# Matmul pieces of 256 and 260 columns in place of equal pieces, results contiguous in PSUM

## The chip, the core and the metric

The kernel runs on one core of one Trainium2 chip. Its engines are TensorE (PE, matmuls into PSUM), VectorE (DVE), ScalarE (ACT), GpSimd (POOL) and SyncE (SP, which issues most DMAs). The metric is the device time of one execution in microseconds (us), the median of three runs.

## What is computed

One layer of a hybrid decoder for 1024 prompt tokens and 8 sample tokens, 1032 token columns in all, model width 1024. Cut to its products:

```python
xn = rmsnorm(x, norm_mix_w)
sc_b, sc_c, sc_x, z, xbc, dt_raw, q, gates = split(xn @ w_in)      # 12320 columns
y_a = (sc_b * conv3(sc_c * sc_x)) @ w_sc_out                       # gated convolution
y_b = group_rmsnorm(ssd(conv4(xbc), dt) * silu(z)) @ w_ssm_out     # state-space scan
y_c = attention(q, mem_k, mem_v) @ w_attn_o                        # 256 memory tokens
x   = x + (g_a*y_a + g_b*y_b + g_c*y_c) @ w_merge_o                # g = sigmoid(gates)
x   = x + (silu(rmsnorm(x) @ w_gate) * (rmsnorm(x) @ w_up)) @ w_down   # hidden width 2816
y   = rmsnorm(x)
```

New caches, convolution histories and scan states are outputs too.

## The kernel before

Activations are kept transposed: 128 features on the partitions, the 1032 tokens as columns. In a product a 128x128 block of weights is the stationary operand and token columns are the moving one. Every fp32 operand is split into a high and a low part of the type fp32r, and a product is three matmuls: high by high, high by low, low by high. PSUM tiles are declared here in banks of 512 fp32 per partition, and each matmul of this kernel writes into one bank.

There are two ways to multiply.

*Plain blocks.* `gemm` (L195 on) makes one block of 128 output features for all 1032 tokens: over 8 values of k, three products each, and for each product three matmuls of CW = 344 columns, one into each bank of a tile of three (`ps[:, n, :CW]`, L214). `flat(ps)` reads the result as three runs of 344, and the SBUF operand beside it is cut the same way by `t3`. It serves two blocks of z, the eight of q and the 32 output projections (`out_part`, and the loop at L1784 on).

*Strassen blocks.* Most of `w_in`, gate, up and most of down go by pairs of output blocks as 2x2 Strassen products with 7 multiplications (`strassen`, L313 on). The second dimension of the 2x2 form is the token axis: the 1032 tokens are two halves of HT = 516. `st_prod` (L256) makes one product: 4 values of k, three products, and for each two matmuls of HC = 258 columns (L262), the first into one bank and the second into the next. The sums of token blocks (`xforms`, `forms`) are made ahead; `forms` tiles hold two halves of 516 side by side, so a half starts 0 or 2064 bytes into its tile. ACT and DVE take each result out of PSUM (`put`, L329 and L331; L364, L368, L377, L379, L384; and the callers' last step), reading it as two runs of 258 with `hv` and cutting the SBUF operand alike with `h3`.

The merge (L1865) and the part of down that is left over from the pairs (L2075) use plain sums over k, but by halves of 516, so also two matmuls of 258. In the merge's last tile (half 1, m = 7) the two pieces have a PSUM tile each: first all 24 matmuls of the first piece run, then all 24 of the second, and each is added to the residual when it is done.

Order of the work: one product follows the other on PE in program order. Small steps of other work are put into queues (`pend`, run by `tick`) and taken at fixed points between products: the scan (L1003 to L1085), the sample tokens' states (L944 to L950), the attention. The stages are: norm, transposes and the first blocks (to 60 us), z, gates, xBC and the short convolution as Strassen blocks (to 990 us), the scan and the attention between plain blocks of q and the output projections (to 1651 us), the merge (to 1745 us), the feed-forward part (to about 2390 us), and the last rows. The file names weights blocks after their use: X for xBC, C and B for the short convolution, G for gates, Z for z, g and u for gate and up.

```python
T = 1024
TT = T + NS            # 1032
CW = TT // NCH         # 344
HT = TT // 2           # 516
HC = HT // 2           # 258
```

Of the kernel before, what the change touches and what calls it, by code (L numbers as in the profile page):

```python
# [11 lines left out]
AF = mybir.ActivationFunctionType  # L12
# [31 lines left out]
def tile_kernel(ctx: ExitStack, tc, a, o):  # L44
# [150 lines left out]
    def gemm(w, acts, name, width=P, off=0):  # L195

        hi, lo = w
        ps = mm_ps(name)
        nk = len(acts)
        n = int(pace[0] + pace[1])  # L200
        pace[1] += pace[0] - n
        marks = [nk * i // n for i in range(n)]
        between = seam.pop() if seam else None
        for k, (ah, al) in enumerate(acts):
            if between is not None:
                between(k)
            if k == 1 and owed:
                owed.pop()()
            for _ in range(marks.count(k)):
                tick()  # L210
            ks = slice(k * width + off, k * width + off + P)
            for i, (wt, x) in enumerate(((hi, ah), (hi, al), (lo, ah))):
                for n in range(NCH):
                    PE.matmul(  # L214
                        ps[:, n, :CW], wt[:, ks], x[:, n * CW : (n + 1) * CW],
                        start=(k == 0 and i == 0), stop=(k == nk - 1 and i == 2),
                    )
        return ps
# [15 lines left out]

    def h3(t):
        return t.rearrange("p (n c) -> p n c", n=2)

    def hv(ps):
        return ps[:, :2, :HC]

# [15 lines left out]
    def st_prod(forms, ps, w, off, f, start):  # L256
        for kt in range(4):
            xh, xl = forms[f][kt]
            ks = slice(off + kt * P, off + (kt + 1) * P)
            for i, (wt, x) in enumerate(((w[0], xh), (w[0], xl), (w[1], xh))):  # L260
                for n in range(2):
                    PE.matmul(  # L262
                        ps[:, n, :HC], wt[:, ks], x[:, n * HC : (n + 1) * HC],
                        start=(start and kt == 0 and i == 0), stop=(kt == 3 and i == 2),
                        skip_group_check=True,
                    )

    def st_early(blocks, forms):


        for first in range(0, len(blocks), 3):
            held = []
            for i, (src1, nm, out, keep) in enumerate(blocks[first : first + 3]):
                wA = st_split(st_raw(src1, f"{nm}Er"), f"{nm}E")
                ps = st_ps(f"m{i}", f"{nm}e")
                o1 = out()
                st_prod(forms, ps, wA, 0, "B11", True)
                S.copy(h3(o1[:, HS[1]]), hv(ps))
                held.append((wA, ps, o1, keep))
            for wA, ps, o1, keep in held:  # L280
                st_prod(forms, ps, wA, 512, "B21", False)
                S.copy(h3(o1[:, HS[0]]), hv(ps))
                keep(o1)
# [29 lines left out]
    def strassen(src1, src2, forms, nm, sums, outs, early=None, after_t3=None, ready=None, hook=None, add=False, begun=None, mid=None):  # L313
# [47 lines left out]
        if early is None:  # L361
            put(o12, pa)
            prod(pc, wA, 512, "B21", True)
            V.tensor_tensor(h3(o11), hv(pc), h3(o11), op=ALU.add)  # L364
        else:
            S.copy(o21, o12)
            V.tensor_sub(o22, o22, o12)
            freed[0] = V.tensor_tensor(h3(o12), hv(pa), h3(o12), op=ALU.add).ins  # L368
        if mid is not None:
# [5 lines left out]
        if after_t3 is not None:  # L375
            after_t3()
        V.tensor_tensor(h3(o22), h3(o22), hv(pa), op=ALU.subtract)  # L377
        prod(pb, wT, 512, "B22", False)
        V.tensor_tensor(h3(o12), h3(o12), hv(pb), op=ALU.subtract)  # L379
        tick()  # L380
        wD = st_split(raw2[:, 512:], f"{nm}D", 512)
        prod(pa, wD, 0, "T4", False)
        if early is not None:
            V.tensor_tensor(h3(o21), hv(pa), h3(o21), op=ALU.add)  # L384
            return o21
# [411 lines left out]
    def sc_pairs(ct):  # L797

        accs = []
        for i in (ct, ct + 1):  # L800
# [12 lines left out]
            ux = u[:, 2 : 2 + TT]  # L813
            V.scalar_tensor_tensor(h3(ux[:, HS[0]]), pa, -1.0, h3(c[:, HS[0]]), op0=ALU.mult, op1=ALU.mult)
            V.tensor_mul(ux[:, HS[1]], ux[:, HS[1]], c[:, HS[1]])
# [16 lines left out]
        SY.dma_start(sc_d[ct], a1)  # L832
        V.scalar_tensor_tensor(h3(a2[:, HS[0]]), pa, -1.0, h3(a2[:, HS[0]]), op0=ALU.mult, op1=ALU.mult)
        V.tensor_mul(a2[:, HS[1]], a2[:, HS[1]], o[1][:, HS[1]])
        SY.dma_start(sc_d[ct + 1], a2)

    def q_step(i):
        def s():
            ps = proj(C_Q + i * P, f"q{i}")
            t = ev_tile(f"q{i}")  # L840
            S.activation(t3(t), flat(ps), AF.Copy, scale=QS)
# [17 lines left out]
    def xbc_pair(c1, c2, after_t3=None):  # L859
# [10 lines left out]
        xbc_conv(c1, us[0], f"x{c1}")  # L870
        S.activation(h3(us[1][:, 3 : 3 + HT]), pa, AF.Copy, scale=-1.0)  # L871
        xbc_conv(c2, us[1], f"x{c2}")

    def z_step(i):
        ps = proj(C_Z + i * P, f"z{i}")
        t = ev_tile(f"z{i}")
        S.activation(t3(t), flat(ps), AF.Silu)
        S.dma_start(zs_d[i], t[:, :TT])

    def plain_pair(col, dst, i, nm, func, hook=None, after_t3=None):  # L880
# [13 lines left out]
        S.activation(os[1][:, HS[1]], os[1][:, HS[1]], func)  # L894
        ins = S.activation(h3(os[1][:, HS[0]]), pa, func, scale=-1.0).ins
        S.dma_start(dst[i + 1], os[1][:, :TT])
# [573 lines left out]
    def out_part(i, m, w, src, nxt):  # L1470
# [14 lines left out]
        if i == 0:  # L1485
            V.tensor_mul(t3(gt), flat(ps), t3(gt))
            owed.append(lambda: SY.dma_start(mg_d[m], gt[:, :TT]))
        elif i == 1:
            t = ev_tile(f"yr{nm}")
            S.copy(t3(t), flat(ps))  # L1490
            S.dma_start(yr_d[m], t[:, :TT])
        else:
            V.tensor_tensor(t3(t), flat(ps), t3(t), op=ALU.add)  # L1493
            V.tensor_mul(t[:, :TT], t[:, :TT], gt[:, :TT])
# [289 lines left out]
    for m in range(KD):  # L1784
# [10 lines left out]
        V.tensor_add(merged[m], merged[m], yg[:, :TT])  # L1795
        V.tensor_mul(t3(gt), flat(ps), t3(gt))  # L1796
        V.tensor_add(merged[m], merged[m], gt[:, :TT])
# [49 lines left out]
    for half in range(2):  # L1847
        sq = ev_tile(f"sq{half}")
        for m in range(KD):
# [7 lines left out]
            def merge_part(out, ns):  # L1857
                for k, (ah, al) in enumerate(mg):
# [3 lines left out]
                    for i, (wt, x) in enumerate(((wh, ah), (wh, al), (wl, ah))):  # L1862
                        for n in ns:
                            c = half * HT + n * HC
                            PE.matmul(  # L1865
                                out[:, n - ns[0], :HC], wt[:, ks], x[:, c : c + HC],
                                start=(k == 0 and i == 0), stop=(k == KD - 1 and i == 2),
                            )

            if half == 1 and m == KD - 1:  # L1870

                for n in range(2):
                    ps = sm_ps(f"pm{half}{m}{n}")
                    merge_part(ps.unsqueeze(1), (n,))
                    c = slice(n * HC, (n + 1) * HC)
                    V.tensor_tensor(t[:, c], ps[:, :HC], xt[:, c], op=ALU.add)
            else:
                ps = mm_ps(f"pm{half}{m}")
                merge_part(ps, (0, 1))
                V.tensor_tensor(h3(t), hv(ps), h3(xt[:, :HT]), op=ALU.add)  # L1880
            if m == 0:
# [65 lines left out]
    def hidden_pair(nm, j, j2):  # L1947
# [18 lines left out]
        )  # L1966
        return o[0], o[1], pa if e is None else h3(pa)

# [6 lines left out]
    for n, (j, j2) in enumerate(pairs):  # L1975
        s1, s2, pa = hidden_pair("g", j, j2)
        S.activation(s1, s1, AF.Silu)
        S.activation(s2[:, HS[1]], s2[:, HS[1]], AF.Silu)
        S.activation(h3(s2[:, HS[0]]), pa, AF.Silu, scale=-1.0)
# [3 lines left out]
        V.scalar_tensor_tensor(h3(s2[:, HS[0]]), pa, -1.0, h3(s2[:, HS[0]]), op0=ALU.mult, op1=ALU.mult)  # L1983
        if j2 != j + 4:
# [53 lines left out]
    def down_pairs(part, fs, begun):  # L2038
        for m in range(0, KD, 2):
# [4 lines left out]
            )  # L2044
            o21 = h3(x2[m + 1][:, HS[0]])
            V.tensor_tensor(o21, o21, pa, op=ALU.subtract)
# [7 lines left out]
    for part, js in enumerate(([0], [9, 10])):  # L2054
# [10 lines left out]
        for m in range(KD):  # L2065
            if not part:
                x2[m] = big(f"x3_{m}")
            for half in range(2):
                ps = st_ps(tags[(2 * m + half) % 3], f"pd{part}{m}{half}")
                for k, (ah, al) in enumerate(hl):  # L2070
                    ks = slice(k * cols + m * P % cols, k * cols + m * P % cols + P)
                    wh, wl = ws[m * P // cols]
                    for i, (wt, x) in enumerate(((wh, ah), (wh, al), (wl, ah))):
                        for n in range(2):
                            PE.matmul(  # L2075
                                ps[:, n, :HC], wt[:, ks], x[:, half * HT + n * HC : half * HT + (n + 1) * HC],
                                start=(k == 0 and i == 0), stop=(k == len(hl) - 1 and i == 2),
                            )
                t = h3(x2[m][:, HS[half]])
                if part:  # L2080
# [186 lines left out]
```

## Time and profile before

| | us |
|---|---|
| time, median of 3 runs | 2445.45 (2445.1 to 2446.07) |
| span of the profiled execution | 2443.0 |
| median above the span | 2.45 |

No other time is listed for the profiled execution than its span, from the first to the last instruction. In the views, L262 is line 262 of the kernel; a row of the timeline has the start, the length, the engine, the line and what is written from what, with the shape of stationary and moving operand; a row of the chain has the start, the length and what it consists of; a row of the busy view by stretch has the stretch, its length, then busy us and (x instructions) of each engine, the granted clock, the share of the DMA engines and GB/s. The length of a matmul in the records includes its way through the array, and neighbours overlap.

### The profile page before, as it was taken

The page shows a single profiled execution, that of the slowest core. Times are in us where ns is not written, and L with a number is a line of the kernel's source. Part 1 is how long each engine was busy: PE and PEld are TensorE (multiplying, and loading weights), DVE is VectorE, ACT ScalarE, POOL GpSimd, SP SyncE. Part 2 cuts the span into 40 slices and gives each one's busy share as a digit, 9 for nine tenths or more (in the row PEclk, how much of TensorE's full clock was granted, in tenths as well). Part 3 has the DMA queues.
Part 4 walks back from the last instruction along what each step waited for, and adds up shares of the span by engine and source line. Part 5 has one row for each costly group of instructions (what it writes and reads, how often), then busy time and mean ns, then how long its engine had stood idle before and what let it go on. Part 6 is the DMA issues. An engine that isn't in the chain of part 4 may idle for free.

```text
span 2443.0 us, 45185 instructions
## 1 busy us (share of the span) xinstructions
PE 2416.7 (99%) x18716; PEld 2343.5 (96%) x18716; DVE 1613.6 (66%) x2597; ACT 1093.6 (45%) x1740; POOL 107.3 (4%) x163
## 2 busy tenths in 40 slices
PE   8999999999999999999999999999999999999998
PEld 6999999999999999998898998999999999999998
DVE  6744677777777676568687773554777655567955
ACT  6633555455453543646555542213543333343423
POOL 0000000000000000212112000000000000000000
PEclk9999999999999999999999999999999999999999
DMA  6354423444353345768887797855445333354622
GB/s 210 128 156 159 135 81 112 139 139 130 104 160 114 100 139 165 234 206 273 259 283 219 258 342 236 281 191 157 156 160 173 106 91 109 87 180 150 191 86 80
DMA packets 357717, 407.94 MB, mean 167 GB/s; under 512 B 16271, under 2 KB 277503, under 8 KB 357504
## 3 DMA queue, kind: packets, MB, share of 16 engines
q1 hardware_dynamic: 334374, 341.79, 45.1%
q10 hardware_dynamic: 23137, 63.26, 6.8%
q8 instruction: 147, 2.41, 0.4%
q14 instruction: 59, 0.48, 0.1%
HBM read 288.85 MB, written 116.38 MB: 166 GB/s over the span
## 4 chain that ended last, share of the span: by engine, by line
PE 89%; DMA 5%; DVE 3%; ACT 2%; issue 1%; SPq 0%; ACTq 0%; DVEq 0%
PE po L214 12%; PE pm L1865 4%; PE ps_q L214 3%; PE pss L1072 1%; PE py L1059 1%; PE ps_z L214 1%; PE po L1051 1%; PE G16m L262 1%; PE G22m L262 1%; PE Z2m L262 1%; PE Z14m L262 1%; PE C1m L262 1%; PE G20m L262 1%; PE C7m L262 1%; PE G12m L262 1%
## 5 line engine op out<-in xcount | busy, mean ns | idle before, releaser
L1003 ACT ACTIVATE r<-r,acum 128x128 f32<-128x128 f32 x256 | 79.2, 391 | 3.8 <-DMA r<-ac_d 3.1
L792 DVE SCALAR_TENSOR_TENSOR ax<-u,prm,ax 128x1024 f32<-128x1024 f32 x44 | 56.3, 1281 | 0.0
L944 ACT ACTIVATE st<-st,es 128x128 f32<-128x128 f32 x128 | 41.2, 391 | 20.9 <-DMA st<-in_state_ssm_dram 12.9
L1036 POOL TENSOR_TENSOR xdd<-xdt,decst 128x512 f32<-128x512 f32 x32 | 34.4, 1074 | 286.5 <-DVE xdt L1032 280.7
L1030 DVE TENSOR_TENSOR r<-r,cbm 128x1024 f32<-128x1024 f32 x32 | 39.1, 1223 | 4.3 <-ACT r L1005 2.4
L946 DVE SCALAR_TENSOR_TENSOR st<-sr,dts,st 128x128 f32<-128x128 f32 x128 | 40.1, 345 | 0.4
L1055 DVE TENSOR_TENSOR y<-po,ea 128x512 f32<-128x512 f32 x28 | 19.3, 690 | 31.0 <-PE po L1051 30.9
L1072 PE MATMUL pss<-xdd,bT 128*128 128x512 f32 x64 | 34.4, 619 | 2.0 <-ACT bT L1029 2.0
L950 DVE SCALAR_TENSOR_TENSOR sr<-st,sr 128x128 f32<-128x128 f32 x128 | 35.3, 285 | 1.1
L1493 DVE TENSOR_TENSOR yr<-po,yr 128x1032 f32<-128x1032 f32 x8 | 9.9, 1232 | 39.1 <-PE po L214 39.1
L1059 PE MATMUL py<-r,xdt 128*64 128x128 f32 x512 | 35.0, 279 | 0.0
L1005 ACT ACTIVATE r<-r 128x1024 f32<-128x1024 f32 x32 | 33.9, 1058 | 0.7
L1085 POOL TENSOR_TENSOR s<-s,cdec 128x512 f32<-128x512 f32 x28 | 33.2, 1185 | 0.7 <-DVE s L1078 0.4
L1880 DVE TENSOR_TENSOR x<-pm,xT 128x516 f32<-128x516 f32 x15 | 10.4, 693 | 33.3 <-PE pm L1865 33.3
L1796 DVE TENSOR_TENSOR gt<-po,gt 128x1032 f32<-128x1032 f32 x8 | 9.9, 1234 | 32.7 <-PE po L214 32.7
L1059 PEld LDWEIGHTS py<-r,xdt 128*64 128x64 f32 x512 | 27.3, 136 | 4.2 <-issue 0.9
L1051 PE MATMUL po<-bc,s 128*128 128x128 f32 x224 | 29.5, 274 | 0.0
L1051 PEld LDWEIGHTS po<-bc,s 128*128 128x128 f32 x224 | 28.3, 191 | 0.0
L795 DVE SCALAR_TENSOR_TENSOR ax<-u,prm,ax 128x1032 f32<-128x1032 f32 x22 | 28.3, 1287 | 0.0
L1596 DVE SCALAR_TENSOR_TENSOR kc<-kc,qb 128x256 f32<-128x256 f32 x64 | 23.8, 419 | 6.5 <-DMA qb<-qs_d 6.5
L1608 ACT ACTIVATE pr<-psa,mx 128x256 f32<-128x256 f32 x32 | 14.9, 471 | 29.2 <-DVE mx L1606 29.2
L789 ACT ACTIVATE ax<-u,prm 128x1024 f32<-128x1024 f32 x22 | 27.4, 1246 | 1.2 <-ACT u L871 0.4
(9245 smaller groups left out, 9047.2 us busy)
## 6 DMA issues: line engine op xcount, KB each, us to landing
r<-ac_d SPq DMA_DIRECT2D x32, 512.0 KB
gt_d<-G ACTq DMA_DIRECT2D x24, 516.0 KB
gt<-gt_d SPq DMA_DIRECT2D x24, 516.0 KB
xs_d<-ax ACTq DMA_DIRECT2D x22, 516.0 KB
zs<-zs_d SPq DMA_DIRECT2D x16, 516.0 KB
yb_d<-x SPq DMA_DIRECT2D x16, 516.0 KB
in<-yb_d SPq DMA_DIRECT2D x16, 516.0 KB
st<-in_state_ssm_dram SPq DMA_DIRECT2D x32, 256.0 KB
```

Of the source, the lines that this page charges most:

```text
L214: PE.matmul(ps[:, n, :CW], wt[:, ks], x[:, n * CW : (n + 1) * CW], start=(k == 0 and i == 0), stop=(k == nk - 1 and i == 2),)
L262: PE.matmul(ps[:, n, :HC], wt[:, ks], x[:, n * HC : (n + 1) * HC], start=(start and kt == 0 and i == 0), stop=(kt == 3 and i == 2), skip_g ...
L792: V.scalar_tensor_tensor(acc[:, :T], u[:, j : j + T], w[j], acc[:, :T], op0=ALU.mult, op1=ALU.add)
L944: S.activation(st[:, i], st[:, i], AF.Copy, scale=es[:, g * 4 + i, b : b + 1])
L946: V.scalar_tensor_tensor(st[:, i], rb, dts[:, g * 4 + i, b : b + 1], st[:, i], op0=ALU.mult, op1=ALU.add)
L950: V.scalar_tensor_tensor(rb, st[:, i], 1.0, rc, op0=ALU.mult, op1=ALU.mult, accum_out=ys[:, g * 4 + i, b : b + 1],)
L1003: S.activation(r[:, j, :], r[:, j, :], AF.Relu, scale=-1.0, bias=acum[:, c, h : h + 1])
L1030: V.tensor_tensor(r, r, bc(cbm.unsqueeze(1), [P, HPG, P]), op=ALU.mult)
L1051: PE.matmul(po[:, t * P : (t + 1) * P], state["s"][:, t * P : (t + 1) * P], bcg[1][:, cs], start=True, stop=True,)
L1059: PE.matmul(py[hp : hp + 64, (h // 2) * P : (h // 2 + 1) * P], xdt[:, h * 64 : (h + 1) * 64], r[:, (h % 2) * 4 + h // 2, :], start=True, s ...
L1072: PE.matmul(pss, bT, xdd, start=True, stop=True)
L1865: PE.matmul(out[:, n - ns[0], :HC], wt[:, ks], x[:, c : c + HC], start=(k == 0 and i == 0), stop=(k == KD - 1 and i == 2),)
```

## The change

Halves of 516 tokens become matmuls of 256 and 260 columns. Their results lie side by side in PSUM: the first in columns 256 to 511 of a bank, the second in columns 0 to 259 of the next, so that 516 columns follow one another without a gap. Plain blocks become matmuls of 260, 512 and 260 columns; their results lie in columns 252 to 511 of the first bank, the whole second bank and columns 0 to 259 of the third, also without a gap. ACT and DVE read each result as one run of 516 or 1032 columns, and the SBUF operands beside it are no longer cut into pieces. In the merge's last tile the two pieces are 256 and 260 columns, still in a PSUM tile each.

```diff
+    THIRDS = ((252, 0, 260), (512, 260, 772), (1024, 772, TT))
+
     def flat(ps):
-        return ps[:, :, :CW]
-
-    def t3(t, lo=0):
-        return t[:, lo : lo + TT].rearrange("p (n c) -> p n c", n=NCH)
+        return ps.rearrange("p n c -> p (n c)")[:, 252 : 252 + TT]
+
+    def thirds(ps, x):
+        f = ps.rearrange("p n c -> p (n c)")
+        for at, lo, hi in THIRDS:
+            yield f[:, at : at + hi - lo], x[:, lo:hi]
...
             for i, (wt, x) in enumerate(((hi, ah), (hi, al), (lo, ah))):
-                for n in range(NCH):
-                    PE.matmul(
-                        ps[:, n, :CW], wt[:, ks], x[:, n * CW : (n + 1) * CW],
-                        start=(k == 0 and i == 0), stop=(k == nk - 1 and i == 2),
-                    )
+                for po, xc in thirds(ps, x):
+                    PE.matmul(po, wt[:, ks], xc, start=(k == 0 and i == 0), stop=(k == nk - 1 and i == 2))
...
-    def h3(t):
-        return t.rearrange("p (n c) -> p n c", n=2)
+    HALF = ((0, 256), (256, HT))
 
     def hv(ps):
-        return ps[:, :2, :HC]
+        return ps.rearrange("p n c -> p (n c)")[:, 256 : 256 + HT]
+
+    def halves_of(ps, x, at=0):
+        f = hv(ps)
+        for lo, hi in HALF:
+            yield f[:, lo:hi], x[:, at + lo : at + hi]
...
             for i, (wt, x) in enumerate(((w[0], xh), (w[0], xl), (w[1], xh))):
-                for n in range(2):
+                for po, xc in halves_of(ps, x):
                     PE.matmul(
-                        ps[:, n, :HC], wt[:, ks], x[:, n * HC : (n + 1) * HC],
-                        start=(start and kt == 0 and i == 0), stop=(kt == 3 and i == 2),
+                        po, wt[:, ks], xc, start=(start and kt == 0 and i == 0), stop=(kt == 3 and i == 2),
                         skip_group_check=True,
                     )
...
             if add:
-                V.tensor_tensor(h3(o), hv(ps), h3(o), op=ALU.add)
+                V.tensor_tensor(o, hv(ps), o, op=ALU.add)
             else:
-                S.copy(h3(o), hv(ps))
+                S.copy(o, hv(ps))
...
-                for n in range(2):
-                    ps = sm_ps(f"pm{half}{m}{n}")
-                    merge_part(ps.unsqueeze(1), (n,))
-                    c = slice(n * HC, (n + 1) * HC)
-                    V.tensor_tensor(t[:, c], ps[:, :HC], xt[:, c], op=ALU.add)
+                for n, (lo, hi) in enumerate(HALF):
+                    ps = sm_ps(f"pm{half}{m}{n}")[:, : hi - lo]
+                    merge_part([ps], (n,))
+                    V.tensor_tensor(t[:, lo:hi], ps, xt[:, lo:hi], op=ALU.add)
...
-                        for n in range(2):
-                            PE.matmul(
-                                ps[:, n, :HC], wt[:, ks], x[:, half * HT + n * HC : half * HT + (n + 1) * HC],
-                                start=(k == 0 and i == 0), stop=(k == len(hl) - 1 and i == 2),
-                            )
+                        for po, xc in halves_of(ps, x, half * HT):
+                            PE.matmul(po, wt[:, ks], xc, start=(k == 0 and i == 0), stop=(k == len(hl) - 1 and i == 2))
```

Every other edit drops `h3` or `t3` around an operand of an eviction. The sums of squares (L1816) and the group means (L1173) keep pieces of 258 and 344.

More of the change, by code (lines that the diff above doesn't have):

```diff
@@ L277, in st_early @@
                 st_prod(forms, ps, wA, 0, "B11", True)
-                S.copy(h3(o1[:, HS[1]]), hv(ps))
+                S.copy(o1[:, HS[1]], hv(ps))
                 held.append((wA, ps, o1, keep))
@@ L281, in st_early @@
                 st_prod(forms, ps, wA, 512, "B21", False)
-                S.copy(h3(o1[:, HS[0]]), hv(ps))
+                S.copy(o1[:, HS[0]], hv(ps))
                 keep(o1)
@@ L363, in strassen @@
             prod(pc, wA, 512, "B21", True)
-            V.tensor_tensor(h3(o11), hv(pc), h3(o11), op=ALU.add)
+            V.tensor_tensor(o11, hv(pc), o11, op=ALU.add)
         else:
@@ L367, in strassen @@
             V.tensor_sub(o22, o22, o12)
-            freed[0] = V.tensor_tensor(h3(o12), hv(pa), h3(o12), op=ALU.add).ins
+            freed[0] = V.tensor_tensor(o12, hv(pa), o12, op=ALU.add).ins
         if mid is not None:
@@ L376, in strassen @@
             after_t3()
-        V.tensor_tensor(h3(o22), h3(o22), hv(pa), op=ALU.subtract)
+        V.tensor_tensor(o22, o22, hv(pa), op=ALU.subtract)
         prod(pb, wT, 512, "B22", False)
-        V.tensor_tensor(h3(o12), h3(o12), hv(pb), op=ALU.subtract)
+        V.tensor_tensor(o12, o12, hv(pb), op=ALU.subtract)
         tick()
@@ L383, in strassen @@
         if early is not None:
-            V.tensor_tensor(h3(o21), hv(pa), h3(o21), op=ALU.add)
+            V.tensor_tensor(o21, hv(pa), o21, op=ALU.add)
             return o21
@@ L840, in s @@
             t = ev_tile(f"q{i}")
-            S.activation(t3(t), flat(ps), AF.Copy, scale=QS)
+            S.activation(t[:, :TT], flat(ps), AF.Copy, scale=QS)
             G.tensor_copy(qs[:, i, :], t[:, T:TT])
@@ L870, in xbc_pair @@
         xbc_conv(c1, us[0], f"x{c1}")
-        S.activation(h3(us[1][:, 3 : 3 + HT]), pa, AF.Copy, scale=-1.0)
+        S.activation(us[1][:, 3 : 3 + HT], pa, AF.Copy, scale=-1.0)
         xbc_conv(c2, us[1], f"x{c2}")
@@ L876, in z_step @@
         t = ev_tile(f"z{i}")
-        S.activation(t3(t), flat(ps), AF.Silu)
+        S.activation(t[:, :TT], flat(ps), AF.Silu)
         S.dma_start(zs_d[i], t[:, :TT])
@@ L1485, in out_part @@
         if i == 0:
-            V.tensor_mul(t3(gt), flat(ps), t3(gt))
+            V.tensor_mul(gt[:, :TT], flat(ps), gt[:, :TT])
             owed.append(lambda: SY.dma_start(mg_d[m], gt[:, :TT]))
@@ L1489, in out_part @@
             t = ev_tile(f"yr{nm}")
-            S.copy(t3(t), flat(ps))
+            S.copy(t[:, :TT], flat(ps))
             S.dma_start(yr_d[m], t[:, :TT])
         else:
-            V.tensor_tensor(t3(t), flat(ps), t3(t), op=ALU.add)
+            V.tensor_tensor(t[:, :TT], flat(ps), t[:, :TT], op=ALU.add)
             V.tensor_mul(t[:, :TT], t[:, :TT], gt[:, :TT])
@@ L1795, in tile_kernel @@
         V.tensor_add(merged[m], merged[m], yg[:, :TT])
-        V.tensor_mul(t3(gt), flat(ps), t3(gt))
+        V.tensor_mul(gt[:, :TT], flat(ps), gt[:, :TT])
         V.tensor_add(merged[m], merged[m], gt[:, :TT])
@@ L1862, in merge_part @@
                     for i, (wt, x) in enumerate(((wh, ah), (wh, al), (wl, ah))):
-                        for n in ns:
-                            c = half * HT + n * HC
+                        for n, po in zip(ns, out):
+                            lo, hi = HALF[n]
                             PE.matmul(
-                                out[:, n - ns[0], :HC], wt[:, ks], x[:, c : c + HC],
+                                po, wt[:, ks], x[:, half * HT + lo : half * HT + hi],
                                 start=(k == 0 and i == 0), stop=(k == KD - 1 and i == 2),
@@ L1870, in tile_kernel @@
             if half == 1 and m == KD - 1:
-                for n in range(2):
-                    ps = sm_ps(f"pm{half}{m}{n}")
-                    merge_part(ps.unsqueeze(1), (n,))
-                    c = slice(n * HC, (n + 1) * HC)
-                    V.tensor_tensor(t[:, c], ps[:, :HC], xt[:, c], op=ALU.add)
+                for n, (lo, hi) in enumerate(HALF):
+                    ps = sm_ps(f"pm{half}{m}{n}")[:, : hi - lo]
+                    merge_part([ps], (n,))
+                    V.tensor_tensor(t[:, lo:hi], ps, xt[:, lo:hi], op=ALU.add)
             else:
                 ps = mm_ps(f"pm{half}{m}")
-                merge_part(ps, (0, 1))
-                V.tensor_tensor(h3(t), hv(ps), h3(xt[:, :HT]), op=ALU.add)
+                merge_part([hv(ps)[:, lo:hi] for lo, hi in HALF], (0, 1))
+                V.tensor_tensor(t, hv(ps), xt[:, :HT], op=ALU.add)
             if m == 0:
@@ L1966, in hidden_pair @@
         )
-        return o[0], o[1], pa if e is None else h3(pa)
+        return o[0], o[1], pa
     PARTS = (1, 11)
@@ L2044, in down_pairs @@
             )
-            o21 = h3(x2[m + 1][:, HS[0]])
+            o21 = x2[m + 1][:, HS[0]]
             V.tensor_tensor(o21, o21, pa, op=ALU.subtract)
@@ L2073, in tile_kernel @@
                     for i, (wt, x) in enumerate(((wh, ah), (wh, al), (wl, ah))):
-                        for n in range(2):
-                            PE.matmul(
-                                ps[:, n, :HC], wt[:, ks], x[:, half * HT + n * HC : half * HT + (n + 1) * HC],
-                                start=(k == 0 and i == 0), stop=(k == len(hl) - 1 and i == 2),
-                            )
-                t = h3(x2[m][:, HS[half]])
+                        for po, xc in halves_of(ps, x, half * HT):
+                            PE.matmul(po, wt[:, ks], xc, start=(k == 0 and i == 0), stop=(k == len(hl) - 1 and i == 2))
+                t = x2[m][:, HS[half]]
                 if part:
```

10 lines of the change are left out of this document (5 added, 5 removed).

## The prediction

> **What bounds the kernel now.** I read first the busy shares and the shares of the chain of work that ended last.
>
> ```profile
> span 2443.0 us, 45185 instructions
> ...
> PE 2416.7 (99%) x18716; PEld 2343.5 (96%) x18716; DVE 1613.6 (66%) x2597; ACT 1093.6 (45%) x1740; POOL 107.3 (4%) x163
> ...
> PEclk9999999999999999999999999999999999999999
> ...
> PE 89%; DMA 5%; DVE 3%; ACT 2%; issue 1%; SPq 0%; ACTq 0%; DVEq 0%
> ```
>
> PE is busy for 99% of the span at the full granted clock, and makes up 89% of the chain. A busy PE need not be a PE at its peak, so I then read the chain in order of time, where an unbroken PE piece (start, length, tile, line, matmuls) means that nothing else held PE up, and the longest wait of PE.
>
> ```profile
> 645.34 20.29 PE X8m L262 x168
> 665.63 20.29 PE G8m L262 x168
> ...
> 1571.92 79.69 PE po L214 x503
> ```
>
> ```profile
> PE ps_B L593 <- ACT xnh L519: 2.8, 3, 1.5
> ```
>
> One Strassen block (7 products of 24 matmuls, 168 in all) follows the next without a gap, each 20.29 us long whether it feeds a convolution (X8) or a gate (G8). PE's longest total wait is 2.8 us, in the opening. So the time is set by how long one matmul after another takes on PE, and a change of a nanosecond per matmul is seen at once: it only has to be multiplied. How many matmuls the diff touches stands in the busy view of the whole span, filtered by the four lines L262, L214, L1865 and L2075 in this order (the number behind x):
>
> ```profile
> 0.00:2443.00 2443.00, 1467.54 (x12096) 1.00 0.52 167
> ...
> 0.00:2443.00 2443.00, 525.74 (x3024) 1.00 0.52 167
> ...
> 0.00:2443.00 2443.00, 93.05 (x768) 1.00 0.52 167
> ...
> 0.00:2443.00 2443.00, 36.07 (x288) 1.00 0.52 167
> ```
>
> L262, L1865 and L2075 are halves of 516 tokens, as two matmuls of 258: (12096 + 768 + 288)/2 = 6576 pairs. L214 is whole blocks of 1032 tokens, as three of 344: 3024/3 = 1008 triples. Busy sums can't be used for the price of one, because neighbouring matmuls overlap in the records; I use the distance from start to start.
>
> **What a matmul of each width costs.** The rows below are from the timeline of PE (start, length, line); each pair is the first and the last start of an unbroken run of one width. The last row of a run is the instruction that comes after it.
>
> ```profile
> 48.43 0.28 PE L595 MATMUL ps_B<-xnh,wl 128*128 128x264 f32 x1
> ...
> 49.17 0.27 PE L512 MATMUL ps_xt<-ident,x 128*128 128x128 f32 x1
> ```
>
> ```profile
> 129.03 0.39 PE L1332 MATMUL ps_kv<-wkv02h,memh 128*128 128x512 f32 x1
> ...
> 131.83 0.28 PE L262 MATMUL Z4m<-T40ah,Z4Dh 128*128 128x258 f32 x1
> ```
>
> ```profile
> 1389.74 0.28 PE L1690 MATMUL psa<-kTh,q11h 128*128 128x256 f32 x1
> ...
> 1390.80 0.32 PE L214 MATMUL po<-b04h,wo15h 128*128 128x344 f32 x1
> ```
>
> ```profile
> 2391.86 0.34 PE L2224 MATMUL pl<-h19h,wl0h 128*128 128x392 f32 x1
> ...
> 2394.00 0.34 PE L2224 MATMUL pl<-h21h,wl0h 128*128 128x392 f32 x1
> ```
>
> ```profile
> 2419.69 0.34 PE L2224 MATMUL pl<-h20h,wl3h 128*128 128x384 f32 x1
> ...
> 2421.27 0.27 PE L2140 MATMUL psy<-ident,x 128*128 128x128 f32 x1
> ```
>
> 256 columns: 9 matmuls in 1.06 us, 117.8 ns each. 264: 6 in 0.74, 123 (the times are rounded to 10 ns, so about 2 either way). 384: 9 in 1.58, 175.6. 392: 12 in 2.14, 178.3. 512: 12 in 2.80, 233.3. The widths 256, 384 and 512 lie on one straight line: 117.8 + 0.451 ns for each further column gives 175.5 and 233.3. On that line 258 columns would be 118.7 and 260 would be 119.6. The blocks above take 20.29/168 = 120.8 for 258, 2.1 over the line. For 344 the run at 1571.92 gives 79.69/504 = 158.1 (seven gemms of 72; one record of the 504 is missing), where the line has 157.5: 0.6 over.
>
> So 258 is the one width that is clearly dearer than its neighbours. Why? Two things are odd in it: 258 is no multiple of 4, and the second piece starts 1032 bytes in, 8 bytes off a multiple of 16. One place in the kernel separates these. In the last tile of the merge (half 1, m = 7) all 24 first pieces run, then all 24 second pieces:
>
> ```profile
> 1739.09 0.28 PE L1865 MATMUL pm<-mgs0h,wm17h 128*128 128x258 f32 x1
> ...
> 1741.97 0.29 PE L1865 MATMUL pm<-mgs0h,wm17h 128*128 128x258 f32 x1
> ...
> 1744.85 0.28 PE L262 MATMUL g0e<-B110h,g0Eh 128*128 128x258 f32 x1
> ```
>
> 24 pieces that start 2064 bytes in, a multiple of 16, take 2.88 us; 24 that start 3096 bytes in, 8 off, take 2.88 us: 120.0 ns each, alike. The start does not matter there; the width does, by 1.3 over the line. The other 0.8 appears only where first and second pieces alternate.
>
> **The change part by part.** Instructions, weight loads, DMAs and waits stay the same in number and order: 24 matmuls in a product, nine per k in a plain block. Nothing is added to any queue, no wait comes in and none goes.
>
> *Halves as 256 + 260.* Now 2 x 120.8 = 241.5 a pair (20.29/84). After it, 256 costs 117.8 by its row. No 260 is in the trace. Fast end: 260 on the line, 119.6, a pair of 237.4, 4.1 less. Slow end: 260 is as far over the line as 258 is (121.7), and 256 too pays the 0.8 of alternating pieces: 118.6 + 121.7 = 240.3, 1.2 less. Between them I take 120.8 for 260, just what 258 costs today, since 258 and 264 (123) enclose it and the nearest row is 258's, and 117.8 for 256: 238.6, 2.9 less. 6576 x 2.9 = **19.1 us** less (ends 27.0 and 7.9).
>
> The Trainium skill's page "SBUF — State Buffer" (Specifications) gives SBUF lines of 16 bytes, of which each new one costs something. The equal halves of the merge's last tile agree with that: 258 columns touch 65 such lines from either start. It is weighed as a rival below.
>
> *Plain blocks as 260 + 512 + 260.* Now 3 x 158.1 = 474.3. After: 512 is 233.3 and 260 between 119.6 and 121.7, so 472.5 to 476.7; with 120.8, 474.9. That is 0.6 x 1008 = 0.6 us more at full count (ends -1.8 and +2.4), and part of these blocks stand in the stage before 1571 us, mixed with the scan and the attention, where the DMA pieces of the chain lie. I take **0**.
>
> *Contiguous results.* DVE and ACT now read PSUM as two runs of 258; after it one run of 516 across two banks. The groups by shape, 516 from PSUM in two runs and 512 in one:
>
> ```profile
> L1880 DVE TENSOR_TENSOR x<-pm,xT 128x516 f32<-128x516 f32 x15 | 10.4, 693 | 33.3 <-PE pm L1865 33.3
> L1055 DVE TENSOR_TENSOR y<-po,ea 128x512 f32<-128x512 f32 x28 | 19.3, 690 | 31.0 <-PE po L1051 30.9
> ```
>
> 693 against 690 ns with 4 columns more: two runs cost nothing to begin with, so little can be won, and one run over two banks is not in the trace. PE hides it: both lines wait for PE, not PE for them. If the cover went, 3 ns on each of some 500 evictions would be 1.5 us. I take 0.
>
> *What is late next.* With PE faster, DVE comes closest in the blocks that carry the convolutions (first row); the next block has room (second row: DVE's busy us behind the length).
>
> ```profile
> 421.73:442.02 20.29, 20.19 (x46) 1.00 0.54 157
> 442.02:462.31 20.29, 12.55 (x36) 1.00 0.51 157
> ```
>
> A block would shrink by 84 x 2.9 ns = 0.24 us. DVE's 20.19 then exceeds its block by 0.14 us and makes it up in the next, which has 7.5 us free. If all eight blocks of this kind (four X and four B blocks that carry convolutions) kept their 0.24, that would be 2 us, inside my ends.
>
> **The sum** goes against the profiled span: 2443.0 - 19.1 = 2423.9 us. No other time of the profiled execution is given. The median of the three runs, 2445.45, lies 2.45 above its span, and I keep that: **2426.4 us**. All terms at their ends: -28.8 gives 2416.6; -7.9 + 2.4 + 2 gives 2442.
>
> **The rivals.**
> *Lines of 16 bytes only.* A piece costs by the groups of four columns that it touches and nothing else, so 260 costs as 258 and 256 one group less. A pair falls from 130 groups to 129: 241.5/130 = 1.86 ns, x 6576 = 12.2 us; triples stay at 258 groups. 2445.45 - 12.2 = 2433.2. For it: the equal halves in the merge's last tile. Against it: by it 256 would cost 120.8 x 64/65 = 118.9, and its row has 117.8. The page named above has such lines. Chance 0.22.
> *Only the sum of columns counts.* 516 columns in two matmuls stay 516 in two; then nothing moves, 2445.45. For it: 256 and 512 lie on one line. Against it: 258 lies 2.1 off that line. The skill's page "TensorE: Matmul & The Clock Gate" (Back-to-back issue gap) has the gap as columns/2.4 + 2.5 ns, which is this rival; the trace disagrees with its size, 233.3 against 215.8 for 512. Chance 0.12.
> *The two pieces no longer write the same columns of their banks* (slower). Today both write columns 0 to 257 of a bank; after the change 256 to 511 of one and 0 to 259 of the next. If each turn then costs the 2.9 ns that I expect to win per pair, the gain is gone at 1.45 ns a piece; at 3 ns a piece (about the distance between 264 and 260 on the rows above) the pairs lose 6.0 - 2.9 = 3.1, x 6576 = 20 us: 2466. Against it: L1690 writes 256 columns into the upper half of a bank at the 117.8 above, though without turning. Chance 0.09.
> My own forecast has the rest, 0.57.
>
> **How the numbers follow.** The likeliest is 2426.4, with 2417 to 2442 as its own range. The range has to reach the unchanged 2445.45, since leaving out that and the slower rival would leave out 0.21; the slower rival stays out. So 2416 to 2446. About 0.2% (4.9 us) is what a measurement of this kernel can tell from no change. Faster: 0.57 + 0.22, less 0.02 for the slow end of my own range: 0.77. Same: 0.12 + 0.02 = 0.14. Slower: 0.09.
>
> **What would show it.** A block of 168 matmuls at 20.04 us in place of 20.29 shows the main term; 20.14 speaks for the lines of 16 bytes, 20.29 for the sum of columns, over 20.4 for the turn between columns. The run of plain blocks from 1571.92 should keep its 79.7 us within 0.5. PE's waits should stay under 3 us each and evictions at 690 ns. I would be wrong if 260 columns cost well over the 121.7 of my slow end, if 256 did not fall below 118.6 where pieces alternate, or if PE, once faster, waits for DVE in the blocks with convolutions.

## The result, and the profile after

| | before | after |
|---|---|---|
| time, median, beside each other on one chip | 2445.76 us (2445.1 to 2446.59, 4 runs) | 2425.8 us (2423.44 to 2428.33, 4 runs) |
| span of the profiled execution | 2443.0 us | 2426.6 us |

The ratio is 0.9923, with an interval from 0.9908 to 0.9937: 18.8 us less by the ratio, 20.0 by the medians. The forecast was 2426.4 us.

The page of the changed kernel, the span, the busy shares and the granted clock:

```profile
span 2426.6 us, 45180 instructions
...
PE 2397.0 (99%) x18716; PEld 2279.9 (94%) x18716; DVE 1613.8 (67%) x2597; ACT 1091.9 (45%) x1740; POOL 106.9 (4%) x163
...
PEclk9999999999999999999999999999999999999999
```

PE still bounds the kernel. It has as many matmuls as before and is busy for 19.7 us less; the span is 16.4 us shorter, so PE's idle time grew from 26.3 to 29.6 us. DVE and ACT are as busy as before. The counts of PE, DVE, ACT and POOL are those of before.

The chain of the changed kernel in order of time (start, length, what): first the run of plain blocks after the attention, then two feed-forward blocks. Behind it, for comparison, stand the same two feed-forward blocks of the kernel before; the second of these is broken after 49 matmuls, so only the first can be compared:

```profile
1564.42 79.39 PE po L218 x503
...
1898.61 19.96 PE g4m L267 x168
1918.57 19.96 PE u4m L267 x168
```

```profile
1908.99 20.21 PE g4m L262 x168
1929.21 5.88 PE u4m L262 x49
```

An unbroken block of 168 matmuls falls from 20.21 to 19.96 us in the feed-forward part. For X8 and G8, which the prediction showed at 20.29, a second profile of the changed kernel (after_again, below) has the chain:

```profile
640.18 20.02 PE X8m L267 x168
660.20 20.02 PE G8m L267 x168
```

20.02 was to be read against 20.04 (the forecast), 20.14 (lines of 16 bytes), 20.29 (only the sum of columns) and over 20.4 (a price of the turn). The plain run goes from 79.69 to 79.39.

The evictions, in the groups of the changed kernel, do not notice that their PSUM operand is one run over two banks:

```profile
L1059 DVE TENSOR_TENSOR y<-po,ea 128x512 f32<-128x512 f32 x28 | 19.3, 690 | 31.3 <-PE po L1055 31.3
...
L1883 DVE TENSOR_TENSOR x<-pm,xT 128x516 f32<-128x516 f32 x15 | 10.4, 694 | 32.3 <-PE pm L1869 32.3
```

694 ns where there were 693.

**Where the time came from.** Averaged from start to start over all records of the Strassen line (breaks left out), the 258 of before cost 119.1 ns as first piece and 122.1 as second, 241.2 a pair. Now 256 costs 117.9 and 260 costs 120.2, 238.1 a pair: 3.1 less, times 6576 pairs, 20.4 us. A plain triple fell from 473.5 to 471.5, 2.0 us over all 1008. Together 22.4 us, of which 16 to 20 arrive. Cut at the same matmuls in both traces, the Strassen stage (about 294 to 990 us of before) is 9.9 us shorter, the feed-forward stage 7.6, z 1.9 and the merge 1.0; but the stage of scan and attention between them is longer. The stretch, its length and PE's busy time, before and after:

```profile
988.20:1569.60 581.40, 573.22 (x3971) 524.81 (x3970) 385.65 (x599) 292.15 (x581) 72.56 (x68) 1.00 0.78 256
```

```profile
977.30:1562.10 584.80, 573.12 (x3970) 490.32 (x3969) 385.50 (x600) 291.44 (x581) 71.03 (x68) 1.00 0.77 254
```

This stage holds no pairs; it should have gained its share of the 2 us of the triples, and it took 3.4 us more, all of it PE without work. The chain of the changed kernel shows on what it hangs there:

```profile
1480.92 4.66 DMA vc<-in_cache_mem_v_dram
...
1496.37 6.68 DMA at_d<-ot
...
1556.28 5.74 DMA in<-at_d
```

These are transfers of the attention, and the change edits none of them. The chain of before has the first and the last of them and not the middle one:

```profile
1490.21 5.84 DMA vc<-in_cache_mem_v_dram
...
1563.38 6.14 DMA in<-at_d
```

contig258, below, has the middle one too (5.81 us), with the old widths, so the change is not needed to bring it. Even so the stage does not look independent of the change. Cut at the same two matmuls, it is 0.3 to 3.4 us longer than before in all six kernels whose pairs are faster (the change and after_again, halves_only, w260, w252_ord and after_ordbef below), and between 2.2 us shorter and 0.7 longer in the four where they are not (contig258, al258, off256, plain_only). That would fit a stage that hangs on transfers and gives back part of what was won ahead of it; one profile of each kernel is not enough to show it.

### The profile page after: what moved, and what is told of

The parts are those of the page before. It is cut to its first block, busy times and chain, and to the rows that moved or that the text cites. A ratio compares the mean times of both kernels' runs of the same rounds, so it can differ in the third digit from the quotient of the medians.

```text
span 2426.6 us, 45180 instructions
## 1 busy us (share of the span) xinstructions
PE 2397.0 (99%) x18716; PEld 2279.9 (94%) x18716; DVE 1613.8 (67%) x2597; ACT 1091.9 (45%) x1740; POOL 106.9 (4%) x163
## 5 line engine op out<-in xcount | busy, mean ns | idle before, releaser
L948 ACT ACTIVATE st<-st,es 128x128 f32<-128x128 f32 x128 | 41.3, 392 | 19.1 <-DMA st<-in_state_ssm_dram 14.5
L1055 PE MATMUL po<-bc,s 128*128 128x128 f32 x224 | 29.6, 275 | 0.0
```

Source lines behind the costliest of these rows:

```text
L948: S.activation(st[:, i], st[:, i], AF.Copy, scale=es[:, g * 4 + i, b : b + 1])
L1055: PE.matmul(po[:, t * P : (t + 1) * P], state["s"][:, t * P : (t + 1) * P], bcg[1][:, cs], start=True, stop=True,)
```

## The experiments

All times are medians, with the kernel before on the same chip beside them (2444.81, 2445.01 and 2445.99 us in the three groups). "Pair" is the mean from start to start of a first and a second piece. "Groups" counts the groups of four columns, 16 bytes, counted from the start of the row, that the two pieces touch.

| kernel | pieces (start of the second) | groups | pair, ns | median, us | ratio, interval |
|---|---|---|---|---|---|
| before | 258 + 258 (258) | 65 + 65 | 241.2 | | |
| contig258 | 258 + 258 (258), results contiguous | 65 + 65 | 241.2 | 2446.16 | 1.0006 [0.9996, 1.0015] |
| al258 | 258 + 258 (256) | 65 + 65 | 241.0 | 2444.17 | 1.0001 [0.9992, 1.0010] |
| off256 | 256 + 260 (254) | 64 + 66 | 242.0 | 2448.9 | 1.0013 [1.0003, 1.0022] |
| plain_only | 258 + 258, plain 260, 512, 260 | 65 + 65 | 241.2 | 2445.33 | 1.0003 [0.9994, 1.0013] |
| halves_only | 256 + 260 (256), plain 344 x 3 | 64 + 65 | 238.3 | 2426.96 | 0.9928 [0.9913, 0.9943] |
| after_again | 256 + 260 (256) | 64 + 65 | 238.1 | 2428.15 | 0.9932 [0.9917, 0.9947] |
| w260 | 260 + 256 (260) | 65 + 64 | 238.3 | 2428.96 | 0.9939 [0.9923, 0.9956] |
| w252 | 252 + 264 (252) | 63 + 66 | 238.0 | 2753.54 | 1.1261 [1.1241, 1.1282] |
| w252_ord | 252 + 264, order of after | 63 + 66 | 238.0 | 2427.62 | 0.9924 [0.9911, 0.9938] |
| before_ord252 | 258 + 258, order of w252 | 65 + 65 | 241.2 | 2764.25 | 1.1300 [1.1285, 1.1316] |
| after_ordbef | 256 + 260, order of before | 64 + 65 | 238.3 | 2430.2 | 0.9937 [0.9923, 0.9950] |

### The parts alone: halves_only, plain_only, contig258

halves_only keeps the plain blocks as they were:

```diff
     def flat(ps):
-        return ps.rearrange("p n c -> p (n c)")[:, 252 : 252 + TT]
+        return ps[:, :, :CW]
...
-        for at, lo, hi in THIRDS:
-            yield f[:, at : at + hi - lo], x[:, lo:hi]
+        for n in range(NCH):
+            yield ps[:, n, :CW], x[:, n * CW : (n + 1) * CW]
```

> Only the halves become 256 + 260 contiguous columns; plain blocks stay three pieces of 344. A Strassen block of 168 matmuls took 20.29 us before and 20.02 to 20.05 after the whole change. If the gain is the halves', blocks are at 20.03 and the time is 6576 pairs x 3.1 ns = 20 us below before (2425 to 2427). Rival, the plain blocks brought part of it: then the kernel is only 12 to 16 us below before.

2426.96 us, a ratio of 0.9928 beside 0.9923 for the whole change: the halves alone give the gain, as far as the intervals tell. Their chain has blocks of 20.02 us.

plain_only has the new plain blocks and the old halves.

> Only plain blocks change, to 260 + 512 + 260; halves stay 258 + 258. My forecast for this part was 0 (-1.8 to +2.4 us). The starts in the changed kernel's trace add up to 471.5 ns a triple against 473.5, which would be 1008 x 2.0 = 2 us less where nothing else holds PE. Rival: the changed pieces disturb the stage of scan and attention, where the profiled run gave back some 4 us; then this kernel is 2 to 4 us slower than before.

2445.33 us, no change that can be told. In its records a plain triple costs 2.0 ns less, and PE is busy for 1.7 us less (2415.0 against 2416.7); the 2 us that this makes over 1008 triples did not arrive in the time, or not visibly.

contig258 has the old widths and the new layout of the results, plain blocks as before:

```diff
-    HALF = ((0, 256), (256, HT))
+    HALF = ((0, 258), (258, HT))
 
     def hv(ps):
-        return ps.rearrange("p n c -> p (n c)")[:, 256 : 256 + HT]
+        return ps.rearrange("p n c -> p (n c)")[:, 254 : 254 + HT]
```

> Pieces stay 258 + 258, but the results lie contiguous in PSUM (columns 254 to 511 of one bank, 0 to 257 of the next) and are read as one run. If layout makes the gain, blocks take 20.03 us and the time is some 20 us below before; if width or start in SBUF make it, blocks stay at 20.29 and the time within 3 us of before.

2446.16 us, and the same 241.2 ns a pair: the layout in PSUM is worth nothing, neither to PE nor to the evictions. It also takes away the turn between columns as a cause, since here, too, the pieces write different columns of their banks.

### Width or start: al258, off256, w260

al258 is contig258 with the second piece read from column 256, so that both pieces start at a multiple of 16 bytes and stay 258 wide:

```diff
-            yield f[:, lo:hi], x[:, at + lo : at + hi]
+            at_x = at + (lo and 256)
+            yield f[:, lo:hi], x[:, at_x : at_x + hi - lo]
```

> Pieces of 258 + 258 columns with contiguous results, but the second piece reads its operand from column 256 (1024 bytes in, a multiple of 16) in place of 258 (1032 bytes): it takes two columns twice and leaves out the last two, in the Strassen blocks and the remainder of down. If the start off a multiple of 16 bytes is what costs, blocks take 20.03 us. If a piece costs by its width, or by the groups of four columns that it touches (65 + 65, as before), blocks stay at 20.29.

off256 is halves_only with the second piece, 260 wide, read from column 254 by the same edit, 8 bytes off. Both kernels read two columns twice and leave out the last two, so they compute something else; only their times are of use.

> Pieces of 256 + 260 columns, contiguous, plain blocks as before, but the second piece reads its operand from column 254 (1016 bytes in, 8 off a multiple of 16) in place of 256: it takes two columns twice and leaves out the last two, in the Strassen blocks and the remainder of down. Width alone: blocks at 20.03 us as in the changed kernel. Start alone: 20.29. Groups of four columns touched (64 + 66 = 130, as before the change): 20.29.

Neither wins anything. The chains (al258 first, then off256):

```profile
644.85 20.42 PE X8m L268 x168
665.27 20.21 PE G8m L268 x168
```

```profile
645.77 20.33 PE X8m L268 x168
666.09 20.33 PE G8m L268 x168
```

Two blocks of al258 take 40.63 us where two of before take 40.58; off256 takes 40.66. A good start with the old width gains nothing, and the good widths with a bad start gain nothing. By pieces: in al258 the first costs 120.0 and the second 121.0; in off256 the 256 costs 118.8 and the 260, which now touches 66 groups, 123.2, 3 ns more than the same width from an even start.

w260 exchanges the widths, 260 + 256.

> The whole change with the halves in the other order, 260 + 256; the second piece starts 1040 bytes in, a multiple of 16 but not of 64. Groups of four: 65 + 64 = 129, blocks at 20.03 us. Rival, whole 64-byte lines count: the 256 columns then touch 17 of them like any other piece, and blocks are near 20.29.

2428.96 us, 238.3 ns a pair, blocks of 19.99 us: which piece comes first does not matter.

So what pays is both together: every pair of 129 groups costs 238.0 to 238.3 ns, every pair of 130 groups 241.0 to 242.0, whatever the widths, the starts and the layout of the results. PE's busy time says the same: 2396.6 to 2398.3 us in the kernels of 129 groups whose PE is not held up, 2415.0 to 2419.5 in those of 130. That is how the rival "lines of 16 bytes" sorts the pairs. Its price was wrong: the step is 3 ns and not 1.86.

Two things are not separated by this. A pair of 516 columns has 129 groups exactly when both pieces start and end on the edge of a group, so no kernel here tells one group more from groups that are only partly used. And the count is not all that matters: a plain triple touches 258 groups before and after, and fell by 2.0 ns. The loads of the weights, on the other hand, do not set the step by themselves: every kernel has 18716 of them, and with the same loads ahead of them pieces follow one another at 116.4 to 123.2 ns, as their columns and starts have it.

### The width 252 + 264, and the order of the instructions

By the count of groups 252 + 264 (129 groups) is as good as 256 + 260. w252 is the changed kernel with `HALF = ((0, 252), (252, HT))` and results from column 260 on.

> The whole change with halves of 252 + 264 columns. Groups of four: 63 + 66 = 129, start 1008 bytes in, a multiple of 16: blocks at 20.03 us, as with 256 + 260. Rival, 256 columns (a whole number of 64-byte lines) is the only cheap width: blocks near 20.29.

It takes 2753.54 us, 12.6% longer than before, though its matmuls, where nothing holds them up, come 238.0 ns a pair. PE's waits (in total, times, longest):

```profile
PE G2m L267 <- ACT G L335: 11.0, 2, 9.0
PE B6m L267 <- DVE b L381: 11.0, 1, 11.0
PE G6m L267 <- ACT G L335: 10.9, 2, 8.9
PE G14m L267 <- ACT G L335: 10.5, 2, 8.4
```

PE waits for evictions. What one of those waits for stands in the timeline of ACT in w252, at the wait of G14m:

```profile
980.88 0.59 ACT L335 COPY G<-G14m 128x516 f32<-128x516 f32 x1 [0.45 <-POOL dts L858]
988.13 2.44 ACT L948 ACTIVATE st<-st,es 128x128 f32<-128x128 f32 x8 [6.65 <-DMA st<-in_state_ssm_dram]
990.48 0.60 ACT L254 CAST G14Dh<-G14r 128x512 fp32r<-128x512 f32 x1
990.99 0.58 ACT L335 COPY G<-G14m 128x516 f32<-128x516 f32 x1
```

Eight steps of the sample tokens' states (L948) stand ahead of the copy that frees PE's PSUM tile, and they wait 6.65 us for the load of the state. In the kernel before these steps lie elsewhere. Comparing the built programs, 971 of 2404 positions in DVE's sequence and 538 of 1789 in ACT's differ between w252 and the changed kernel, although the source differs in two lines: the framework orders the instructions of each engine when it builds the program, and that order depends on the widths. The changed kernel differs from the one before, too, in 120 and 67 positions. The sequences of the other engines move as well: PE's in 1016 of 18145 positions between w252 and the changed kernel, and that of SP, which issues DMAs, in 155 of 838.

Two theories were left, order and width. Three kernels exchange the orders: at the end of the program the instructions of every engine are tied into a given sequence, which adds no wait between engines:

```diff
     with _tile.TileContext(nc) as tc:
         tile_kernel(tc, ins, outs)
+        force_order(nc, tc)     # for each engine: each instruction after the one before it in the given list
```

> The widths of w252 (252 + 264), with the instructions of every engine held in the order that the changed kernel (256 + 260) has. Theory 'order': the 12.6% that w252 lost came from the order in which DVE and ACT take their work (971 of 2404 positions of DVE and 538 of 1789 of ACT differed from the changed kernel's); the pair of 252 + 264 was measured at 238.0 ns from start to start, as the changed kernel's 238.1, so the time is 2424 to 2431 us. Theory 'width': 252 or 264 columns themselves, or a piece that starts at column 260 of a bank, make evictions late; then it stays near 2750 us.

> The kernel before (258 + 258, 344 x 3, results in two or three runs), with the instructions of every engine held in w252's order; nothing else differs. Theory 'order': it becomes slow as w252 did; its blocks of 168 matmuls are 0.25 us longer, which takes little off waits of up to 11 us, so 2700 to 2780 us, with PE waiting for ACT and DVE at the blocks' ends. Theory 'width': it stays at 2445 us.

> The changed kernel with the instructions of every engine held in the order of the kernel before (120 of 2404 positions of DVE and 67 of 1789 of ACT are moved back). If the moved positions cost the part of the gain that is missing (pairs 20.4 us and triples 2 us add up to 22.4, of which 17 to 20 arrived), it is faster than the changed kernel, 2423 us. If the order costs nothing here, 2425 to 2428 as the changed kernel, and the missing part is lost in other waits.

The widths 252 + 264 in the changed kernel's order take 2427.62 us, as fast as the change. The old widths in w252's order take 2764.25. So the 12.6% are the order's, all of them, and the width is free. All engines were held at once, so the runs don't show which engine's order it is. The ACT rows for the states, first of before_ord252, then of w252_ord, each with its total wait, times and longest wait:

```profile
ACT st L944 <- DMA st<-in_state_ssm_dram: 60.2, 11, 11.2
```

```profile
ACT st L948 <- DMA st<-in_state_ssm_dram: 19.9, 9, 3.2
```

In w252 the same row has 81.9 us in 13 waits, up to 11.4 us; in the kernel before it has 12.9 in 7, up to 2.6. PE is idle for 253 us of w252 (2752.2 less 2499.2 busy), so these loads are shown as the cause of the one wait above and not of them all.

A wait costs more than its length. In the timeline of PE in w252, each row starts two matmuls, a pair:

```profile
982.55 0.40 PE L267 MATMUL G14m<-xnl,G14Ah 128*128 128x252 f32 x2
982.78 0.40 PE L267 MATMUL G14m<-xnh,G14Al 128*128 128x252 f32 x2
991.62 0.80 PE L267 MATMUL G14m<-xnh,G14Th 128*128 128x252 f32 x2 [8.44 <-ACT G L335]
...
993.09 0.64 PE L267 MATMUL G14m<-xnh,G14Th 128*128 128x252 f32 x2
993.52 0.64 PE L267 MATMUL G14m<-xnl,G14Th 128*128 128x252 f32 x2
...
998.03 0.40 PE L267 MATMUL G14m<-xnh,G14Th 128*128 128x252 f32 x2
998.27 0.40 PE L267 MATMUL G14m<-xnl,G14Th 128*128 128x252 f32 x2
```

Ahead of the wait a pair comes every 0.23 to 0.24 us, after it every 0.43, and only some 6 us later every 0.24 again. The granted clock goes the same way: 1.00 from 960 to 977 us and 0.50 from 988 to 997.5. The Strassen stage of w252 and of w252_ord (stretch, length, PE busy, then among others the granted clock, last but two) shows the sum:

```profile
304.00:1140.00 836.00, 727.73 (x5765) 721.96 (x5765) 501.48 (x959) 332.71 (x493) 15.17 (x82) 0.92 0.36 107
```

```profile
290.00:977.00 687.00, 685.77 (x5768) 684.76 (x5767) 498.65 (x966) 334.00 (x491) 32.13 (x82) 1.00 0.42 129
```

Of 149 us more, 107 are PE without work (108.3 against 1.2) and 42 are longer work on the same matmuls, at a mean granted clock of 0.92. The Trainium skill's page "TensorE: Matmul & The Clock Gate" (HAM oscillation — how this bites in real kernels) tells of this: a wait of several microseconds puts the clock back to half, and the way back is paid again each time; the trace agrees, with 0.43 us a pair after a wait of 8.44 us.

after_ordbef was to tell whether the positions that moved in the change itself cost what is missing of the 22.4 us. It takes 2430.2 us, not 2423, and is even a little over the 2425 to 2428 expected if the order costs nothing: the moves cost nothing that can be told, and the missing part is not the order's.

after_again, the changed kernel once more, was to tell whether its spread of 2423.4 to 2428.3 us comes from the stage of scan and attention. Its profile has that stage 2.6 us shorter than the first one, but the Strassen stage 1.1 us longer (682.7 against 681.6), and both spans are alike (2426.4 and 2426.6): that stage varies, but it alone does not set the spread.

## Why the prediction was right, point by point

The time was right to 0.6 us, and the mechanism half right. Both have a share of luck. PE won 22.4 us where 19.1 were forecast, and 2 to 6 were lost again in stages that the forecast left alone, so two misses cancel in part. And one reading of the trace was wrong, which did no harm only because the change has good widths and a good start at once.

- **PE bounds everything, and a nanosecond per matmul counts 13152 times.** Right: a block fell from 20.29 to 20.02 us and the span with it, though 3.3 us of it came back as idle time of PE.
- **256 + 260 costs 238.6 instead of 241.5, 2.9 ns less.** Measured 238.1 against 241.2, 3.1 less. 256 was priced at 117.8 and has 117.9; 260 was taken at 120.8, as 258 costs, and has 120.2. 19.1 us were forecast, 20.4 are there.
- **"The start does not matter there; the width does."** Wrong as a reading of the cause. The merge's last tile compared 258 from an even start with 258 from 8 bytes off, and both touch 65 groups: the comparison could not separate start from width. off256 does, and the start costs 3 ns there. That the forecast held is luck in this point: the change happens to keep the second piece on a multiple of 16 bytes (256 x 4). By my reading off256, whose widths are those of the change, would cost 238.6 a pair; it costs 242.0.
- **The rival "lines of 16 bytes".** Its count sorts the pairs of all kernels rightly, but its price and its "nothing else" did not stand up. I spread the cost of a pair evenly over its 130 groups, 1.86 ns each. But the pieces measured (252: 116.4, 256: 117.9, 260: 120.2, 264: 121.6 ns) rise by 1.5, 2.3 and 1.4 a group, and pieces with half a group at an end cost more than their count says: 258 with 65 groups has 120.6 on average against 120.2 for 260 with 65, and 260 from 8 bytes off 123.2 against 121.6 for 264, both 66. That 256 was cheaper than the rival's 118.9 therefore spoke against the price only; I had used it against the whole rival. A full group costs 1.7 ns on average over those three steps, so some 1.4 of the 3.1 ns would be left for the two half groups; that is an estimate, and why these cost extra the runs don't show. The triples go against the rule too: 258 groups before and after, and 2.0 ns less.
- **Only the sum of columns counts.** Fell: the sum is 516 in every kernel. **The turn between columns** fell with contig258, which turns and costs 241.2.
- **Plain blocks 0.** Right for the time. Their triple was priced at 0.6 ns more and is 2.0 less (260 at 119.5 to 120.1, 512 at 231.9 in place of 233.3). The run of 504 fell by 0.3 us, within the 0.5 allowed.
- **Contiguous results 0.** Right: 694 against 693 ns, and contig258 at 1.0006.
- **"Instructions … stay the same in number and order."** Wrong in the order: 120 positions of DVE and 67 of ACT moved, and 798 of PE's 18145. It cost nothing that can be told here, as after_ordbef shows, but w252 shows what this step could have cost: a rival of plus 12% that the prediction did not have.
- **DVE late next, up to 2 us.** It did not bite: the Strassen stage, which holds the blocks with convolutions, is 9.9 us shorter, and its 2883 pairs (5767 matmuls from 294 to 990 us of before) times 3.1 ns are 8.9.
- **Waits under 3 us.** Nearly: PE's largest total is 3.1 us, in the scan, in five waits of at most 1.5.

What stays open is where exactly 2 to 6 of the 22.4 us go. The stage of scan and attention, which hangs on transfers, returns 0.5 to 3.4 us in the profiles of halves_only, after_again and the change, 1.0 us is lost at the opening of the changed kernel, and the rest mostly in the feed-forward part; all of it is too small to tell apart from the differences between runs.

## What to carry to other kernels

Cut the moving operand of such matmuls so that every piece starts at a multiple of four columns of fp32 and is a multiple of four columns wide: it cost nothing and gave 3 of 241 ns a pair here. When a trace is to tell whether the start matters, take two rows of one width whose starts make them touch different numbers of groups; two rows that touch equally many say nothing. When a small edit of shapes moves the time by much more than its instructions' prices, compare the order of each engine's instructions first, and hold it fixed before blaming the shape.

## What the runs showed of the hardware that was not expected

A piece of 260 columns costs 120.2 ns from a multiple of 16 bytes and 123.2 from 8 bytes off it. Equal pieces of 258 share their 241 ns unequally, 119.1 and 122.1 before and 120.0 and 121.0 in al258, where both start at a multiple of 16 bytes. The Trainium skill's page "SBUF — State Buffer" (Specifications) has lines of 16 bytes with a price for each new one; the pairs agree with such lines as the unit, 238.0 to 238.3 ns for 129 of them and 241.0 to 242.0 for 130, but the triples, with 258 both times, fell by 2.0 ns, which such lines alone don't explain. 512 columns cost 231.9 ns within the plain triples, where a run of 512 alone had 233.3. After PE had waited 8.44 us its matmuls took nearly twice their time for some 6 us, so that in one stage 107 us more of idle time went with 149 us more in all.
